# The order of two products in each group of a seven-product matmul form

## The chip, the cores and the metric

One core of a Trainium2 chip runs the whole program. Its engines work side by side, each through a list of its own: PE (TensorE, matmuls), DVE (VectorE, elementwise work), ACT (ScalarE, activations and copies), POOL (GpSimd) and SP (SyncE), of which the last two only issue transfers in the part that matters here. The metric is device microseconds of one execution, the median of several; lower is better.

## The reference

A decoder trunk of two layers over 256 tokens of width 2048, all in f32. What this case turns on are its large products with weights. Everything else (a causal convolution, eight attention heads, norms, gates) is left out here:

```python
for i in range(DEPTH):                     # DEPTH = 2
    h = rmsnorm(x, norm_mix_g[i])
    proj = h @ w_in[i]                     # 2048 columns each for the two branch gates, and more
    ...
    merged = jax.nn.sigmoid(g_conv) * y_conv + jax.nn.sigmoid(g_attn) * y_attn
    x = x + merged @ w_out[i]              # 2048 x 2048
    hf = rmsnorm(x, norm_ffn_g[i])
    gate, up = jnp.split(hf @ w_gate_up[i], 2, axis=-1)     # 2048 x 11264
    x = x + (jax.nn.silu(gate) * up) @ w_down[i]            # 5632 x 2048
    hp = rmsnorm(x, norm_ple_g[i])
    x = x + jax.nn.sigmoid(hp @ w_ple_gate[i]) * (p[i] @ w_ple_proj[i])
return rmsnorm(x, final_g)
```

## The kernel before, in words

**Tiles and splits.** Weights come from memory in raw tiles of 128 partitions by 2 x 512 f32 (512 KB, two slices of 128 inputs by 512 output columns), fetched by SP (`fetch`, L135) into eight `raw` buffers. Each f32 weight tile is split into two parts (`split`): ACT copies it in a shorter format to `wh` (L141), and DVE subtracts that from the raw tile, which leaves the rest `wl` (L142). A product of 128 inputs then takes three matmuls (`Sum.add`): inputs' high part by `wh` (L186), high part by `wl` (L187), low part by `wh` (L188). There are five `wh` and five `wl` buffers. The inputs, transposed activations, are split in the same way.

**Sums and banks.** A sum of two token blocks by 512 columns takes two banks of the accumulator, one a block. `bank_mm` gives such a pair, the name `mm` in the rows; there are two pairs, handed out in turn at the first matmul that writes them. `bank_ms` gives single banks (`ms`), of which there are four.

**Two chunks at once.** `fast_chunks` computes two neighbouring chunks of 512 columns, with weights w1 and w2. For some of the input slices (its groups, `fast`; a group is 512 inputs) it uses a form with seven products in place of eight: the two token blocks, the two chunks and the two halves of the 512 inputs form 2 x 2 matrices, the products are taken of sums of them, and the sums of weights are made by DVE on raw tiles in place (L273 adds, L274 subtracts). In the names, a11 and a12 are the first and second half of w1's group, a22 is the second half of w2's, and sm is the sum of the first halves of both, which POOL makes by an adding transfer (L277, `third`). The sums: `chain` and `q5` in single banks, c11 and c12 (token blocks 0 and 1 of the first chunk) in one pair, c21 and c22 (of the second chunk) in the other. The other input slices are multiplied plainly: each `go()` takes one raw tile, splits it and multiplies it into both blocks of the first chunk, c11 and c12, twelve matmuls; the tiles of the second chunk follow those of the first.

**The end of a call.** When all of the first chunk's `go` are done, `add(u1, u1, c1())` (L273, `pair<-pair,mm`) reads its pair and `first(u1)` uses the result. At the very end `sub(u2, c2(), u2)` (L274, `pair<-mm,pair`) reads the pair of the second chunk. The next call takes up both pairs.

**Who calls it.** The branch gates (two groups), `w_out` and `w_ple_gate` (one group for the first two chunks, two for the others), the gate and up columns of the FFN (L937, two groups, a call for each 512 columns of the hidden width but the layer's first), and `w_down` (L951; FFN in three parts per layer of 3, 4 and 4 chunks of the hidden width; one group for `n == 0`, that is columns 0 to 1023, and for `n == 2` as many as the part has `Fast` operands). 84 groups in all.

**The order of the work.** A scheduler takes the instructions as the code writes them and sets an order for each engine; a buffer's next writer waits for its last reader. On each engine the instructions then run in the order set.

Of the kernel before, what the change touches and what calls it, by code (L numbers as in the profile page):

```python
# [45 lines left out]
def trunk(ctx, tc, xT, xR, pT, wI, wF, wC, wA, wOut, wGU, wD, wPG, wPP, vec, bF, gF, out):  # L46
# [15 lines left out]
    def pair(dtype=F32):  # L62
        return pairs.tile([P, 2, 512], dtype, tag="pair", name=f"pair{next(uid)}")
# [20 lines left out]
    def run():  # L84
        for _ in range(len(turns)):
            turns.popleft()()
        if tasks:
            tasks.popleft()()

    def fill(n):  # L90
        credit[0] += n
        while background and credit[0] > 0:
            cost, op = background.popleft()
            credit[0] -= cost
            op()
        if not background:
            credit[0] = 0
# [35 lines left out]
    def fetch(src):  # L133
        raw = raws.tile([P, 2, 512], F32, tag="raw", name=f"raw{next(uid)}")
        nc.sync.dma_start(raw.rearrange("p k n -> p (k n)"), src)  # L135
        return raw

    def split(raw):
        h = whs.tile([P, 2, 512], F32R, tag="wh", name=f"wh{next(uid)}")
        l = wls.tile([P, 2, 512], F32R, tag="wl", name=f"wl{next(uid)}")  # L140
        act.activation(h, raw, AF.Copy)  # L141
        dve.tensor_tensor(l, raw, h.bitcast(F32), op=ALU.subtract)  # L142
        recent[0] = h
        return h, l
# [28 lines left out]
    class Sum:  # L173
# [8 lines left out]
        def add(self, xh, xl, wh, wl):  # L182
            start = self.left == self.n
            self.left -= 1
            kw = dict(skip_group_check=self.rest < self.n)
            pe.matmul(self.t, lhsT=xh, rhs=wh, start=start, stop=False, **kw)  # L186
            pe.matmul(self.t, lhsT=xh, rhs=wl, start=False, stop=False, **kw)  # L187
            pe.matmul(self.t, lhsT=xl, rhs=wh, start=False, stop=self.left % self.rest == 0, **kw)  # L188

    def once(make):  # L190

        made = []

        def get():
            if not made:
                made.append(make())
            return made[0]

        return get

    def sums_of_blocks(n1, n2=None):
        t = once(bank_mm)
        return t, Sum(n1, lambda: t()[:, 0, :]), Sum(n1 if n2 is None else n2, lambda: t()[:, 1, :])

    def plain(sums, xs, k0, parts, blocks=range(2)):
        h, l = parts
        for kk in range(2):
            for b in blocks:
                xh, xl = xs[k0 + kk]
                sums[b].add(xh(b), xl(b), h[:, kk, :], l[:, kk, :])  # L210

    def await_x(xs, ks):
        while not all(k in xs for k in ks):
            assert turns or tasks
            run()
# [24 lines left out]
    def fast_chunks(fast, w1, w2, xs, ks, first, by_block=None):  # L240

        nf, nk = 2 * len(fast), 4 * len(ks)
        chain, q5 = Sum(3 * nf, once(bank_ms), 3), Sum(nf, once(bank_ms))
        c1, c11, c12 = sums_of_blocks(nf + nk)
        c2, c21, c22 = sums_of_blocks(nf + nk, nk)
        if by_block is not None:
            c22 = Sum(nk, once(bank_ms))
        left = deque()  # L250
        for w, sums in ((w1, (c11, c12)), (w2, (c21, c22))):
            for g, k0 in enumerate(ks):
                for half in range(2):
                    left.append((w[len(fast) + g][:, half * 1024 : (half + 1) * 1024], sums, k0 + 2 * half))
        state = dict(quiet=True)

        def go(n=1):
            for _ in range(n):
                src, sums, k0 = left.popleft()
                parts = split(fetch(src))  # L260
                await_x(xs, (k0, k0 + 1))
                plain(sums, xs, k0, parts)
                if not state["quiet"]:
                    fill(CONV // 2 + len(left) % 2)
                    run()

        def product(to, operand, raw):
            h, l = split(raw)
            xh, xl = operand
            for kk in range(2):  # L270
                to.add(xh(kk), xl(kk), h[:, kk, :], l[:, kk, :])

        add = lambda o, a, b: dve.tensor_tensor(o, a, b, op=ALU.add)  # L273
        sub = lambda o, a, b: dve.tensor_tensor(o, a, b, op=ALU.subtract)  # L274
        def third(g):
            sm = fetch(w2[g][:, :1024])
            nc.gpsimd.dma_start(sm.rearrange("p k n -> p (k n)"), w1[g][:, :1024], accum_op=ALU.add)  # L277
            return sm

        s3 = [third(0)]  # L280
        a11s = []
        for g, f in enumerate(fast):
            a11s.append(fetch(w1[g][:, :1024]))
            product(chain, f(B11), a11s[g])
        u1 = pair()
        act.activation(u1[:, 0, :], chain.t, AF.Copy)
        for g, f in enumerate(fast):
            a11, sm = a11s[g], s3[g]
            a22, a12 = fetch(w2[g][:, 1024:]), fetch(w1[g][:, 1024:])
            product(c21, f(N4X), a22)  # L290
            go()
            product(c11, f(B21), a12)
            if len(left) > 2 * len(ks):
                go()
            if nk == 8 and len(fast) == 1:
                run()
            if g < len(fast) - 1:
                s3.append(third(g + 1))
            add(a22, sm, a22)
            product(chain, f(NT2), a22)  # L300
            if g == len(fast) - 1:
                act.activation(u1[:, 1, :], chain.t, AF.Copy)
            sub(a11, a22, a11)
            product(q5, f(M1), a11)
            add(a12, a12, a22)
            product(c12, f(B22), a12)
        for sm, f in zip(s3, fast):
            product(chain, f(T3), sm)
        add(u1[:, 1, :], u1[:, 1, :], q5.t)
        u2 = pair()  # L310
        act.activation(u2[:, 0, :], chain.t, AF.Copy)
        add(u2[:, 1, :], u2[:, 0, :], q5.t)
        state["quiet"] = False
        go(len(left) - 2 * len(ks))
        add(u1, u1, c1())
        first(u1)
        if by_block is None:
            go(len(left))
            sub(u2, c2(), u2)
            return u2  # L320
        go(len(left) - 4)
        held = [(split(fetch(src)), k0) for src, _, k0 in left]
        for b, c in enumerate((c21, c22)):
            for parts, k0 in held:
                plain([c, c], xs, k0, parts, [b])
            sub(u2[:, b, :], c.t, u2[:, b, :])
            by_block(b, u2)
# [28 lines left out]
    B11, B12, B21, B22, M1, NT2, T3, N4X = range(8)  # L356
# [203 lines left out]
    for i in range(L):  # L560
# [296 lines left out]
        def sigmoids(c, nf):  # L857

            ts = []

            def gate(t):
                for b in range(2):
                    act.activation(t[:, b, :], t[:, b, :], AF.Sigmoid, scale=norm.r(b))
                ts.append(t)

            gate(fast_chunks(norm.fast[:nf], wI[i, c], wI[i, c + 1], norm.xs, range(4 * nf, KD, 4), gate))
            return ts
# [38 lines left out]
        for n in range(0, N4, 2):  # L906
            by = (0, 1, 2, 3) if n == 0 else (0, 3, 1, 2)
            onto_x(norm, n + 1)(
                fast_chunks(
                    [fast_merged[g] for g in by[: 1 + n // 2]], *([wOut[i, m][g] for g in by] for m in (n, n + 1)),  # L910
                    merged, [4 * g for g in by[1 + n // 2 :]], onto_x(norm, n),
                )
            )
# [4 lines left out]
        for part, nch in enumerate(FFN_PARTS):  # L918
            hid = {}
            fast_hid = [Fast() for _ in range(nch - 2)]  # L920
            for c in range(c0, c0 + nch):
                w1, w2 = wGU[i, 2 * c], wGU[i, 2 * c + 1]
# [159 lines left out]
```

## Time and profile before

| | |
|---|---|
| median of three runs | 2796.34 us (2795.89 to 2798.07) |
| the profiled execution | 2801.55 us |
| its span, first to last instruction | 2799.8 us |
| granted TensorE clock | 0.997 |
| PE, DVE, ACT, POOL busy | 99%, 88%, 61%, 3% |
| weights and other transfers | 587.36 MB, mean 210 GB/s |

A row of the timeline gives the start in us, the busy time, the engine, the line of the kernel, the operation, what it writes and reads, and in brackets how long the engine was idle before and what it waited for. The names leave the buffers' numbers out. Equal instructions that follow each other stand in one row with their count, and its time runs from the first's start to the last's end. A matmul's end is modelled and overlaps the next one's start, so the pace of PE is read from starts.

### The profile page before, as it was taken

How to read it: one execution, taken by the hardware profiler on the slowest of the kernel's cores; microseconds unless marked ns; L12 is line 12 of the kernel's file. 1: busy time of each engine (PE TensorE's matmuls, PEld its weight loads, DVE VectorE, ACT ScalarE, POOL GpSimd, SP SyncE). 2: the span in 40 equal slices, each digit the busy share in tenths (PEclk: the TensorE clock that was granted, in tenths of full speed). 3: DMA queues.
4: the chain of work that ended last, by engine and by line, in shares of the span. 5: the costliest groups of instructions: out<-in, count | busy, mean ns of one | idle time of the engine just before them, and what ended most of it. 6: DMA issues, size and time to landing. Idle time of an engine off the chain costs nothing.

```text
span 2799.8 us, 35090 instructions
## 1 busy us (share of the span) xinstructions
PE 2772.3 (99%) x12544; PEld 2291.1 (82%) x12544; DVE 2475.0 (88%) x2931; ACT 1716.6 (61%) x2110; POOL 82.2 (3%) x125
## 2 busy tenths in 40 slices
PE   9999999999999999999999999999999999999998
PEld 7888888888888888888788888888887888888786
DVE  7998889878889989988869988988798898899888
ACT  7446666666556656667744466656665566566575
POOL 0000000000000000000000000000000000000000
PEclk9999999999999999999999999999999999999999
DMA  7556566666677667776655555675666777677673
GB/s 299 188 185 194 186 198 219 192 225 195 219 225 228 228 208 232 218 220 232 191 179 189 187 180 198 195 236 180 218 199 224 222 226 238 203 229 217 212 251 123
DMA packets 162176, 587.36 MB, mean 210 GB/s; under 512 B 18256, under 2 KB 18512, under 8 KB 161744
## 3 DMA queue, kind: packets, MB, share of 16 engines
q1 hardware_dynamic: 149040, 539.50, 56.0%
q0 software_dynamic: 12096, 44.05, 9.0%
q8 instruction: 98, 1.61, 0.2%
q10 hardware_dynamic: 864, 1.57, 0.2%
q14 instruction: 78, 0.64, 0.1%
HBM read 582.95 MB, written 2.10 MB: 209 GB/s over the span
## 4 chain that ended last, share of the span: by engine, by line
PE 87%; DVE 5%; DMA 4%; issue 2%; ACT 1%; SPq 0%; POOLq 0%; ACTq 0%; DVEq 0%; POOL 0%
PE mm L186 23%; PE mm L188 23%; PE mm L187 23%; PE ms L186 5%; PE ms L187 5%; PE ms L188 5%; DVE wl L142 3%; DMA raw<-in_wD_dram 2%; PE ms L349 2%; ACT wh L141 1%; DMA raw<-in_wGU_dram 1%; DVE raw L274 1%; DMA raw<-in_wI_dram 0%; PE ms L741 0%; DVE pair L274 0%
## 5 line engine op out<-in xcount | busy, mean ns | idle before, releaser
L141 ACT ACTIVATE wh<-raw 128x1024 fp32r<-128x1024 f32 x1266 | 1313.0, 1057 | 943.2 <-PE mm L188 540.5
L142 DVE TENSOR_TENSOR wl<-raw,wh 128x1024 fp32r<-128x1024 f32 x1266 | 1507.7, 1219 | 250.6 <-ACT wh L141 244.6
L186 PE MATMUL mm<-wh,pair 128*128 128x512 f32 x3184 | 1247.7, 392 | 7.9 <-DVE pair L274 7.4
L187 PE MATMUL mm<-wl,pair 128*128 128x512 f32 x3184 | 1243.0, 390 | 3.5 <-DVE wl L142 3.5
L188 PE MATMUL mm<-wh,pair 128*128 128x512 f32 x3184 | 1241.9, 390 | 0.6 <-DVE pair L340 0.5
L186 PEld LDWEIGHTS mm<-wh,pair 128*128 128x128 f32 x3184 | 598.6, 188 | 132.8 <-ACT wh L141 10.0
L188 PEld LDWEIGHTS mm<-wh,pair 128*128 128x128 f32 x3184 | 598.5, 188 | 127.4 <-DVE pair L340 1.2
L187 PEld LDWEIGHTS mm<-wl,pair 128*128 128x128 f32 x3184 | 598.6, 188 | 127.0 <-DVE wl L142 5.3
L186 PE MATMUL ms<-wh,pair 128*128 128x512 f32 x712 | 277.7, 390 | 0.0
L187 PE MATMUL ms<-wl,pair 128*128 128x512 f32 x712 | 277.1, 389 | 0.0
L188 PE MATMUL ms<-wh,pair 128*128 128x512 f32 x712 | 277.1, 389 | 0.0
L273 DVE TENSOR_TENSOR raw<-raw,raw 128x1024 f32<-128x1024 f32 x168 | 205.0, 1220 | 10.9 <-DMA raw<-in_wD_dram 8.1
L584 DVE SCALAR_TENSOR_TENSOR pair<-pair,vecs,pair 128x256 f32<-128x256 f32 x480 | 201.0, 475 | 0.0
L186 PEld LDWEIGHTS ms<-wh,pair 128*128 128x128 f32 x712 | 133.6, 188 | 28.4 <-ACT pair L1013 0.8
L187 PEld LDWEIGHTS ms<-wl,pair 128*128 128x128 f32 x712 | 133.7, 188 | 27.9 <-DVE wl L142 0.2
L188 PEld LDWEIGHTS ms<-wh,pair 128*128 128x128 f32 x712 | 133.6, 188 | 27.8
L274 DVE TENSOR_TENSOR raw<-raw,raw 128x1024 f32<-128x1024 f32 x84 | 102.5, 1220 | 1.0
L273 DVE TENSOR_TENSOR pair<-pair,ms 128x512 f32<-128x512 f32 x96 | 65.4, 681 | 10.4 <-PE ms L188 10.2
L389 DVE TENSOR_TENSOR pair<-pair,pair 128x1024 fp32r<-128x1024 f32 x52 | 63.0, 1218 | 0.0
L273 DVE TENSOR_TENSOR pair<-pair,mm 128x1024 f32<-128x1024 f32 x48 | 58.3, 1214 | 4.8 <-PE mm L188 4.8
L388 ACT ACTIVATE pair<-pair 128x1024 fp32r<-128x1024 f32 x52 | 54.6, 1059 | 8.8 <-DVE pair L379 8.1
L274 DVE TENSOR_TENSOR pair<-mm,pair 128x1024 f32<-128x1024 f32 (+1 forms) x48 | 57.9, 1206 | 1.9 <-PE mm L188 1.8
(170 smaller groups left out, 1094.7 us busy)
## 6 DMA issues: line engine op xcount, KB each, us to landing
raw<-in_wGU_dram SPq DMA_DIRECT2D x352, 512.0 KB, 5.1
raw<-in_wI_dram SPq DMA_DIRECT2D x287, 512.0 KB, 4.0
raw<-in_wD_dram SPq DMA_DIRECT2D x176, 512.0 KB, 5.7
raw<-in_wOut_dram SPq DMA_DIRECT2D x64, 512.0 KB, 5.0
raw<-in_wPG_dram SPq DMA_DIRECT2D x64, 512.0 KB, 4.9
raw<-in_wGU_dram POOLq DMA_DIRECT2D x40, 512.0 KB, 7.8
raw<-in_wA_dram SPq DMA_DIRECT2D x32, 512.0 KB, 4.8
raw<-in_wC_dram SPq DMA_DIRECT2D x32, 512.0 KB, 5.5
```

What stands on the lines that cost most here:

```text
L141: act.activation(h, raw, AF.Copy)
L142: dve.tensor_tensor(l, raw, h.bitcast(F32), op=ALU.subtract)
L186: pe.matmul(self.t, lhsT=xh, rhs=wh, start=start, stop=False, **kw)
L187: pe.matmul(self.t, lhsT=xh, rhs=wl, start=False, stop=False, **kw)
L188: pe.matmul(self.t, lhsT=xl, rhs=wh, start=False, stop=self.left % self.rest == 0, **kw)
L273: add = lambda o, a, b: dve.tensor_tensor(o, a, b, op=ALU.add)
L274: sub = lambda o, a, b: dve.tensor_tensor(o, a, b, op=ALU.subtract)
L349: pe.transpose(pt[:, kk * S + b * P : kk * S + (b + 1) * P], src(b)[:, c : c + P], ident)
L388: act.activation(h, t, AF.Copy)
L389: dve.tensor_tensor(l, t, h.bitcast(F32), op=ALU.subtract)
L584: dve.scalar_tensor_tensor(cv[c], u[c][:, j : j + S], w, cv[c], op0=ALU.mult, op1=ALU.add,)
```

## The change

Within each group, the product into c11 and one `go()` now stand ahead of the product into c21, and a second `go()`, where there is one, behind it. The two fetches change places with them. What follows (the sum a22, its product NT2, and so on) is as before.

```diff
         for g, f in enumerate(fast):
             a11, sm = a11s[g], s3[g]
-            a22, a12 = fetch(w2[g][:, 1024:]), fetch(w1[g][:, 1024:])
+            a12, a22 = fetch(w1[g][:, 1024:]), fetch(w2[g][:, 1024:])
+            product(c11, f(B21), a12)
+            go()
             product(c21, f(N4X), a22)
-            go()
-            product(c11, f(B21), a12)
             if len(left) > 2 * len(ks):
                 go()
             if nk == 8 and len(fast) == 1:
                 run()
             if g < len(fast) - 1:
                 s3.append(third(g + 1))
             add(a22, sm, a22)
             product(chain, f(NT2), a22)
             ...
             sub(a11, a22, a11)
             product(q5, f(M1), a11)
             add(a12, a12, a22)
             product(c12, f(B22), a12)
```

No instruction is added or removed on any engine; the orders of PE, ACT and DVE differ, and SP loads the two halves in the other order.

PE, at the start of the `w_down` call for columns 0 to 1023 that begins at 722 us of the profile: the end of the first product into a pair and the start of the first `go`. Before, product into c21 (`mm1191`), then the `go` into c11 and c12 (`mm1195`):

```order
L186 MATMUL mm1191_6282<-wh1189_6278,pair1100_5854 128x512
L187 MATMUL mm1191_6282<-wl1190_6279,pair1100_5854 128x512
L188 MATMUL mm1191_6282<-wh1189_6278,pair1101_5855 128x512
L186 MATMUL mm1195_6295<-wh1193_6291,pair1169_6188 128x512
L187 MATMUL mm1195_6295<-wl1194_6292,pair1169_6188 128x512
L188 MATMUL mm1195_6295<-wh1193_6291,pair1169_6188 128x512
```

Now, product into c11, then the `go`:

```order
L186 MATMUL mm1191_6282<-wh1189_6278,pair1098_5850 128x512
L187 MATMUL mm1191_6282<-wl1190_6279,pair1098_5850 128x512
L188 MATMUL mm1191_6282<-wh1189_6278,pair1099_5851 128x512
L186 MATMUL mm1191_6282<-wh1193_6291,pair1169_6188 128x512
L187 MATMUL mm1191_6282<-wl1194_6292,pair1169_6188 128x512
L188 MATMUL mm1191_6282<-wh1193_6291,pair1169_6188 128x512
```

The first product and the first `go` now write the same pair; the second pair is first written by the product into c21 after them.

DVE at the same call. `raw1187` is the tile of the first product, `raw1192` that of the `go`, `raw1188` that of the other product, `raw1181` the sum sm, `raw1182` a11; `pair1164` is the u2 of the call before. Before:

```order
L142 TENSOR_TENSOR wl1190_6279<-raw1187_6274,wh1189_6278 128x1024
L337 TENSOR_TENSOR pair1169_6188<-ms1168_6183,pair1169_6188 128x2x256
L337 TENSOR_TENSOR pair1171_6196<-ms1170_6191,pair1171_6196 128x2x256
L273 TENSOR_TENSOR raw1187_6274<-raw1181_6256,raw1187_6274 128x1024
L142 TENSOR_TENSOR wl1194_6292<-raw1192_6289,wh1193_6291 128x1024
L274 TENSOR_TENSOR raw1182_6259<-raw1187_6274,raw1182_6259 128x1024
L142 TENSOR_TENSOR wl1197_6309<-raw1188_6276,wh1196_6308 128x1024
L273 TENSOR_TENSOR raw1188_6276<-raw1188_6276,raw1187_6274 128x1024
L274 TENSOR_TENSOR pair1164_6159<-mm1124_5953,pair1164_6159 128x1024
L142 TENSOR_TENSOR wl1200_6321<-raw1198_6318,wh1199_6320 128x1024
```

Now:

```order
L142 TENSOR_TENSOR wl1190_6279<-raw1187_6274,wh1189_6278 128x1024
L142 TENSOR_TENSOR wl1194_6292<-raw1192_6289,wh1193_6291 128x1024
L142 TENSOR_TENSOR wl1196_6308<-raw1188_6276,wh1195_6307 128x1024
L273 TENSOR_TENSOR raw1188_6276<-raw1181_6256,raw1188_6276 128x1024
L274 TENSOR_TENSOR pair1164_6159<-mm1130_5982,pair1164_6159 128x1024
L142 TENSOR_TENSOR wl1200_6321<-raw1198_6318,wh1199_6320 128x1024
L939 SCALAR_TENSOR_TENSOR pair1119_5943<-pair1164_6159,rt979_5243,pair1119_5943 128x512 x2
L142 TENSOR_TENSOR wl1206_6354<-raw1188_6276,wh1205_6353 128x1024
L274 TENSOR_TENSOR raw1182_6259<-raw1188_6276,raw1182_6259 128x1024
L273 TENSOR_TENSOR raw1187_6274<-raw1187_6274,raw1188_6276 128x1024
```

Ahead of the previous call's last read of its pair (L274 into `pair1164`) there stood the sum a22, the subtraction a11 and the sum a12; now only the sum a22 does.

DVE in the second group of the gate and up call at 928 us. `raw1526` is the tile of the group's first product, `raw1527` that of the other, `raw1530` and `raw1535` those of the two `go`, `raw1518` the sum sm, `raw1500` a11. Before:

```order
L142 TENSOR_TENSOR wl1529_7915<-raw1526_7910,wh1528_7914 128x1024
L273 TENSOR_TENSOR raw1526_7910<-raw1518_7873,raw1526_7910 128x1024
L142 TENSOR_TENSOR wl1532_7927<-raw1530_7924,wh1531_7926 128x1024
L142 TENSOR_TENSOR wl1534_7943<-raw1527_7912,wh1533_7942 128x1024
L142 TENSOR_TENSOR wl1537_7955<-raw1535_7952,wh1536_7954 128x1024
L142 TENSOR_TENSOR wl1539_7972<-raw1526_7910,wh1538_7971 128x1024
L274 TENSOR_TENSOR raw1500_7797<-raw1526_7910,raw1500_7797 128x1024
L273 TENSOR_TENSOR raw1527_7912<-raw1527_7912,raw1526_7910 128x1024
L142 TENSOR_TENSOR wl1541_7984<-raw1500_7797,wh1540_7983 128x1024
```

Now:

```order
L142 TENSOR_TENSOR wl1529_7915<-raw1526_7910,wh1528_7914 128x1024
L142 TENSOR_TENSOR wl1532_7927<-raw1530_7924,wh1531_7926 128x1024
L142 TENSOR_TENSOR wl1534_7943<-raw1527_7912,wh1533_7942 128x1024
L142 TENSOR_TENSOR wl1537_7955<-raw1535_7952,wh1536_7954 128x1024
L273 TENSOR_TENSOR raw1527_7912<-raw1518_7873,raw1527_7912 128x1024
L274 TENSOR_TENSOR raw1500_7797<-raw1527_7912,raw1500_7797 128x1024
L142 TENSOR_TENSOR wl1539_7972<-raw1527_7912,wh1538_7971 128x1024
L273 TENSOR_TENSOR raw1526_7910<-raw1526_7910,raw1527_7912 128x1024
L142 TENSOR_TENSOR wl1541_7984<-raw1500_7797,wh1540_7983 128x1024
```

The sum a22 (L273 reading `raw1518`) stood second and now stands fifth, behind the splits of the other product's tile and of both `go`; the subtraction a11 has moved ahead of the split for NT2.

## The prediction, made before the changed kernel was run

> **What bounds the kernel.** I read the page's busy shares and the chain that ended last first, then what PE waited for, then the timeline around those waits, and last VectorE (DVE) at the places where the change reorders it. The span, the busy shares, the chain by engine, and three lines of PE's waits:
>
> ```profile
> span 2799.8 us, 35090 instructions
> PE 2772.3 (99%) x12544; PEld 2291.1 (82%) x12544; DVE 2475.0 (88%) x2931; ACT 1716.6 (61%) x2110; POOL 82.2 (3%) x125
> PE 87%; DVE 5%; DMA 4%; issue 2%; ACT 1%; SPq 0%; POOLq 0%; ACTq 0%; DVEq 0%; POOL 0%
> ...
> PE mm L186 <- DVE pair L274: 7.4, 4, 2.1
> PE mm L187 <- DVE wl L142: 3.5, 4, 1.6
> PE ms L349 <- DVE xt L981: 1.3, 1, 1.3
> ```
>
> PE is busy 99% of the span. The change alters no matmul count, so the most it can gain lies in PE's waits. The largest is a wait of the first matmul of a sum (L186 into `mm`) for a subtraction that reads a sum's pair of banks (L274 into `pair`): 7.4 us in four places. The first of the four, at the call of `w_down` for columns 0 to 1023 in layer 0, and then the other three and a smaller wait of the same matmul in a fifth such call:
>
> ```profile
> 726.18 0.39 PE L188 MATMUL mm<-wh,pair 128*128 128x512 f32 x1
> ...
> 727.76 0.39 PE L186 MATMUL mm<-wh,pair 128*128 128x512 f32 x1
> 728.32 1.22 DVE L273 TENSOR_TENSOR raw<-raw,raw 128x1024 f32<-128x1024 f32 x1
> 728.90 0.39 PE L188 MATMUL mm<-wh,pair 128*128 128x512 f32 x1
> 729.46 1.22 DVE L274 TENSOR_TENSOR pair<-mm,pair 128x1024 f32<-128x1024 f32 x1
> 730.82 0.47 PE L186 MATMUL mm<-wh,pair 128*128 128x512 f32 x1 [1.53 <-DVE pair L274]
> ...
> 962.21 0.47 PE L186 MATMUL mm<-wh,pair 128*128 128x512 f32 x1 [1.64 <-DVE pair L274]
> 2122.29 0.58 PE L186 MATMUL mm<-wh,pair 128*128 128x512 f32 x1 [2.14 <-DVE pair L274]
> 2353.86 0.47 PE L186 MATMUL mm<-wh,pair 128*128 128x512 f32 x1 [0.26 <-ACT wh L141]
> 2606.15 0.47 PE L186 MATMUL mm<-wh,pair 128*128 128x512 f32 x1 [2.04 <-DVE pair L274]
> ```
>
> The call before ends its last `go` at 726.18. The chain product follows, and at 727.76 the product into c21 begins: six matmuls, starts 0.228 us apart ((728.90 - 727.76) / 5). A product is thus 6 x 0.228 = 1.36 us of PE, and a `go`, with twelve, 2.72. Then PE stands: the first `go` writes c12, which lies in the pair that c11 shares, and that pair was the previous call's c2, which the subtraction u2 = c2 - u2 (L274, 729.46) has yet to read. That subtraction needs the last matmul of 726.18 only, but DVE runs the subtraction a11, a split and the sum a12 (L273, 728.32) first.
>
> **Gain A: the pair is asked for later.** The new order puts the product into c11 first, then the `go`, both in the pair that comes free early; the other pair is first touched by the product into c21. Between the previous call's last matmul and that first touch PE now has chain 1.36, product 1.36 and `go` 2.72: 5.44 us in place of 2.72. At this call the touch falls at 726.18 + 0.22 + 5.44 = 731.84. The subtraction a11 and the sum a12, 2.28 us of issue, no longer stand ahead of the reading of c2, which I put at 727.3 to 728.5; even at the old 729.46 its 1.22 us would end at 730.7. The cover exceeds the price by over 1 us, so the wait goes whole. A wait counts for the PE starts that it displaces: the last start before it is at 728.90, the next at 730.82, 1.92 instead of 0.23, so 1.69 lost where the row says 1.53; 0.16 more. Four waits: 7.4 + 4 x 0.16 = 8.0; the fifth call gives 0.26 + 0.16 = 0.4. Together 8.4 us. What is late next at these places is nothing that the trace shows: the splits for the `go` are two operations behind the first product. The bounds: no gain if the subtraction is held back beyond 731.84; 8.4 if not. I take 8.4, since less stands ahead of it than before. In `w_ple_gate`, PE waits for the last transposed input:
>
> ```profile
> 1393.57 0.66 PE L349 MATMUL ms<-ident,xt 128*128 128x128 f32 x4 [1.26 <-DVE xt L981]
> ```
>
> That operation is behind the same reading of c2 on DVE, and what moves back there is two operations of 1.14 us of issue (below), against splits that move up: at most 1.26 + 0.16 = 1.4, at least 0; I take 1.2, near the whole. All gains: 9.6 us.
>
> **Loss C: the sum a22 comes later on DVE.** In a call with two groups DVE ran, for the second group, split of a22, sum, split of the `go`'s tile, split of a12, split of the second `go`'s tile, and then the split for NT2, the subtraction, the sum a12 and the split for M1. Now the splits of a12, of the `go`'s tile, of a22 and of the second `go`'s tile come first, and the sum after them. DVE in the gate/up call at 928 us, and the matmul that needs its last split (M1):
>
> ```profile
> 925.75 3.50 DVE L142 TENSOR_TENSOR wl<-raw,wh 128x1024 fp32r<-128x1024 f32 x3
> 929.28 1.22 DVE L273 TENSOR_TENSOR raw<-raw,raw 128x1024 f32<-128x1024 f32 x1
> 930.87 2.36 DVE L142 TENSOR_TENSOR wl<-raw,wh 128x1024 fp32r<-128x1024 f32 x2 [0.36 <-ACT wh L141]
> 934.41 2.36 DVE L142 TENSOR_TENSOR wl<-raw,wh 128x1024 fp32r<-128x1024 f32 x2 [1.18 <-ACT wh L141]
> 936.69 1.22 DVE L274 TENSOR_TENSOR raw<-raw,raw 128x1024 f32<-128x1024 f32 x1
> 937.82 1.22 DVE L273 TENSOR_TENSOR raw<-raw,raw 128x1024 f32<-128x1024 f32 x1
> 939.12 2.36 DVE L142 TENSOR_TENSOR wl<-raw,wh 128x1024 fp32r<-128x1024 f32 x2
> ...
> 940.67 0.39 PE L187 MATMUL ms<-wl,pair 128*128 128x512 f32 x1
> ```
>
> Two splits in a row take 2.36, so one costs 1.14 of issue. DVE stands 1.18 us before 934.41 for ACT's copy of the second `go`'s tile, which itself arrives late: its buffer came free late. In the old order the sum (929.28) was done in front of that idle time; in the new one it is done behind it, and the idle time grows by what the sum leaves. So the splits for NT2 and M1 come 1.14 us later wherever DVE had such a wait. That DVE does not use the wait for something else is seen in the same rows: the subtraction of 936.69 has its operands since the sum of 929.28 ended at 930.50, and it still ran only after both splits. If ready work could pass work that waits, C would be nothing and the sum -9.6 alone; as these rows go, C stands. The Trainium skill, in "Perfetto Trace Analysis", section "Tensor Engine Instruction (MATMUL, LD_WEIGHTS)", says that PE can pull weight loads ahead, while ACT, DVE and GPSIMD are strictly first in, first out. The trace agrees, with the start at 936.69 against operands ready at 930.50, so the rule speaks against this change by the whole of C.
>
> In first groups the sum also moves, but DVE has no such wait there and the work up to M1 is the same: nothing lost; if the a22 sum were late there too, each would cost up to 1.14, which is rival 2. SP and POOL issue in the same places; only which half of the weights is loaded first changes, with 512 KB either way: nothing, since both halves were fetched one behind the other.
>
> How much of 1.14 reaches PE depends on the room between the split's end and the matmul. At 928 us: 939.12 + 1.22 = 940.34, due at 940.67: 0.33. The other late groups (`w_out` of both layers, two calls each of the second gate/up part of layer 0 and of both parts of layer 1):
>
> ```profile
> 470.59 2.36 DVE L142 TENSOR_TENSOR wl<-raw,wh 128x1024 fp32r<-128x1024 f32 x2
> 471.99 0.40 PE L187 MATMUL ms<-wl,pair 128*128 128x512 f32 x1
> 1185.25 0.50 PE L187 MATMUL mm<-wl,pair 128*128 128x512 f32 x1 [0.77 <-DVE wl L142]
> 1861.20 2.36 DVE L142 TENSOR_TENSOR wl<-raw,wh 128x1024 fp32r<-128x1024 f32 x2
> 1862.91 0.39 PE L187 MATMUL ms<-wl,pair 128*128 128x512 f32 x1
> 2331.06 2.36 DVE L142 TENSOR_TENSOR wl<-raw,wh 128x1024 fp32r<-128x1024 f32 x2
> 2333.70 0.39 PE L187 MATMUL ms<-wl,pair 128*128 128x512 f32 x1
> 2582.79 2.36 DVE L142 TENSOR_TENSOR wl<-raw,wh 128x1024 fp32r<-128x1024 f32 x2
> 2584.09 0.47 PE L187 MATMUL ms<-wl,pair 128*128 128x512 f32 x1
> ```
>
> Rooms, by the same subtraction: 0.18, none (PE already waits at 1185), 0.49, 1.42 and 0.08. The busy time of the engines in two of the four stretches between the late calls of a gate/up part (columns: elapsed, then PE, its loads, DVE, ACT, POOL; clock; DMA share):
>
> ```profile
> 893.20:930.60 37.40, 37.40 (x171) 31.02 (x170) 37.12 (x37) 24.93 (x28) 1.70 (x2) 1.00 0.73 220
> 2540.10:2573.90 33.80, 33.80 (x155) 28.05 (x154) 33.64 (x34) 23.58 (x28) 1.71 (x2) 1.00 0.75 227
> ```
>
> DVE has 0.28 and 0.16 us to spare there, so it cannot make up in a stretch what it lost at its start: the lateness of two calls adds up to 2.28 before the room of the second is charged. This gives 1.14 - 0.18 = 1.0 and 1.14 - 0.49 = 0.6 for `w_out`, and for the gate/up parts 2.28 - 0.33 = 1.9, 1.1 (at 1185 PE already waits for a late tile, in which I let the first call's lateness run out, and charge the second's whole), 2.28 - 1.42 = 0.9 and 2.28 - 0.08 = 2.2. Sum 7.7 us. Bounds: nothing, if the buffers that the late tiles wait for come free earlier in the new order by as much; and twice as much, 15.4, if the subtraction and the sum a12 behind the moved sum are each late by a full operation too. I take 7.7, since the rows show the wait for ACT and the order shows the sum behind it.
>
> **The sum.** -9.6 + 7.7 = -1.9 us against the profiled execution, whose own time, 2801.55, stands 5.2 above the median of the runs, 2796.34. Taken from the median: 2794.4. About 0.2% (5.6 us) is what a measurement of this kernel can tell from no change, so I forecast no change that shows.
>
> **Rivals.** First, the lateness is absorbed: the late tiles arrive earlier, because the order of last uses of the raw buffers moves too, or the gate/up parts regain it in the idle time that DVE has elsewhere. For it speaks DVE's busy share of 88%; against it the stretches above, where DVE is full. With 0 to 2 us of C left it gives 2796.34 - 9.6 + 0 to 2 = 2787 to 2789: faster. Chance 0.26.
>
> Second, slower: every second group of the gate/up calls carries the lateness to PE. The groups are counted by the summing transfers, one each, two in a call:
>
> ```profile
> raw<-in_wGU_dram POOLq DMA_DIRECT2D x40, 512.0 KB, 7.8
> ```
>
> So 20 second groups, at the split for M1, 1.14 each: 22.8, with `w_out`'s 1.6 a loss of 24.4 - 9.6 = +14.8, 2811. It shows as slower from a loss of 9.6 + 5.6 = 15.2, when 12 of the 20 pay in full. Against it stand the room of 1.42 at 2331 and that PE waits for splits in four places only (3.5 us, above). Chance 0.08.
>
> Third, the wait at the pair stays: if the subtraction u2 is now held behind more splits, the product into c21 waits as the `go` did. Then A is nothing and C remains: +7.7 - 1.2, 2803. Against it the 5.44 us of cover. Chance 0.04. That the change does nothing on the engines is out: the bank written by the first `go` differs.
>
> **How the numbers follow.** The forecast, no visible change, has 0.62; its own range is 2791 to 2798.5, from the uncertainty of the rooms and of the 1.2. Faster by over 0.2% means under 2790.7: rival one, 0.26, and a little of the forecast's edge: 0.27. Slower by over 0.2% means over 2801.9: rivals two and three, 0.11. The range of eight in ten reaches down into rival one, to 2787.5, and up to 2799.5, short of rival two.
>
> **What would show it.** In the changed kernel's waits the line of L186 for the subtraction L274 should be gone or under 1 us, and the first `go` at the `w_down` calls should follow the product without a pause. PE's waits for splits (L187 for `wl`) should have grown from 3.5 to about 10 us, mostly into `ms`, and DVE's idle time before the second `go`'s split in second groups from about 1.2 to 2.3. If the L187 waits stay near 3.5, rival one holds; if they reach 20, rival two; if L186 still waits 7 us, rival three. The forecast is wrong as a whole if PE's lost time moves by more than 5 us in total.

## The result: slower, and the profile after

The changed kernel takes 2815.07 us (median of 4 runs, 2814.84 to 2815.83), the kernel before 2796.94 in the same comparison: a ratio of 1.0065 with a 95% interval of 1.0048 to 1.0083, 18 us slower. The profiled execution of after took 2814.84 us, its median; that of before lay 5 us above its own, so the two traces differ by 13.3 us of span only. The page of after (span, busy time, the chain by engine, the splits on DVE):

```profile
span 2813.1 us, 35137 instructions
PE 2780.5 (99%) x12544; PEld 2284.9 (81%) x12544; DVE 2475.1 (88%) x2931; ACT 1711.5 (61%) x2110; POOL 82.2 (3%) x125
PE 66%; DVE 18%; DMA 6%; issue 6%; ACT 3%; ACTq 0%; DVEq 0%; SPq 0%; POOLq 0%; POOL 0%
...
L142 DVE TENSOR_TENSOR wl<-raw,wh 128x1024 fp32r<-128x1024 f32 x1266 | 1515.8, 1219 | 276.1 <-ACT wh L141 265.7
```

The row of the splits in the page of before:

```profile
L142 DVE TENSOR_TENSOR wl<-raw,wh 128x1024 fp32r<-128x1024 f32 x1266 | 1507.7, 1219 | 250.6 <-ACT wh L141 244.6
```

PE's waits in after (us in total, times, the longest):

```profile
PE mm L187 <- DVE wl L142: 7.9, 15, 1.4
PE ms L187 <- DVE wl L142: 4.9, 13, 0.6
PE ms L760 <- ACT wh L141: 1.9, 2, 1.2
PE ms L741 <- DVE pair L273: 1.3, 2, 0.9
```

The wait of L186 for L274 (7.4 us in four places) is gone. In its place PE waits for splits 28 times, 12.8 us, where it did so four times, 3.5 us. DVE was idle ahead of its splits for 276.1 us where it was 250.6. It does the same work (2475.0 and 2475.1 us), but its share of the chain has gone from 5% to 18%, DMA's from 4% to 6%, and PE's from 87% to 66%: less of the chain is now PE's own work. PE's busy time grew by 8.2 us with the same 12544 matmuls. A matmul row is 0.39 us long and the next can start 0.23 after it, so the first 0.16 us of a wait do not show as one; they lengthen the busy time, as does the longer row of the matmul behind a wait (0.50 at 938.92, below). The waits' rows add 4.6 us (14.2 before, 18.8 after, with the small lines left out here), and 8.2 + 4.6 is 12.8 of the 13.3 us.

First the gain. The `w_down` call that waited at 730.82 before, in after; the chain product, the reading of the old pair, the product into c11, and the product into c21:

```profile
730.69 0.39 PE L186 MATMUL ms<-wh,pair 128*128 128x512 f32 x1
731.66 1.22 DVE L274 TENSOR_TENSOR pair<-mm,pair 128x1024 f32<-128x1024 f32 x1
732.05 0.39 PE L186 MATMUL mm<-wh,pair 128*128 128x512 f32 x1
...
736.13 0.39 PE L186 MATMUL mm<-wh,pair 128*128 128x512 f32 x1
```

The reading ends at 732.88, and the pair is asked for at 736.13 (1.36 + 2.72 after 732.05): 3.2 us of cover. But here the reading would have been in time for the old order of products too, which asked for the pair 2.72 us after the chain product's start, at 733.41. The reading itself comes earlier: with the subtraction a11 and the sum a12 behind it, DVE starts it 0.97 us after the chain product (731.66 - 730.69), where it was 3.06 before (729.46 against 727.76 - 1.36).

Then the loss. DVE, SP and ACT in the gate/up call that starts at about 910 us. Before, the end of the first group (its second group is in the prediction):

```profile
921.05 2.35 DVE L142 TENSOR_TENSOR wl<-raw,wh 128x1024 fp32r<-128x1024 f32 x2
923.33 1.22 DVE L274 TENSOR_TENSOR raw<-raw,raw 128x1024 f32<-128x1024 f32 x1
924.46 1.21 DVE L273 TENSOR_TENSOR raw<-raw,raw 128x1024 f32<-128x1024 f32 x1
925.75 1.23 DVE L142 TENSOR_TENSOR wl<-raw,wh 128x1024 fp32r<-128x1024 f32 x1
925.75 0.33 SPq L135 DMA_DIRECT2D raw<-in_wGU_dram  x1
927.00 0.33 SPq L135 DMA_DIRECT2D raw<-in_wGU_dram  x1
929.77 2.01 ACT L141 ACTIVATE wh<-raw 128x1024 fp32r<-128x1024 f32 x2 [1.97 <-PE ms L188]
```

and after, the same and the second group:

```profile
926.63 1.21 DVE L142 TENSOR_TENSOR wl<-raw,wh 128x1024 fp32r<-128x1024 f32 x1
927.76 1.21 DVE L273 TENSOR_TENSOR raw<-raw,raw 128x1024 f32<-128x1024 f32 x1
929.01 1.23 DVE L274 TENSOR_TENSOR raw<-raw,raw 128x1024 f32<-128x1024 f32 x1
930.15 1.22 DVE L142 TENSOR_TENSOR wl<-raw,wh 128x1024 fp32r<-128x1024 f32 x1
931.29 1.22 DVE L273 TENSOR_TENSOR raw<-raw,raw 128x1024 f32<-128x1024 f32 x1
932.42 3.65 DVE L142 TENSOR_TENSOR wl<-raw,wh 128x1024 fp32r<-128x1024 f32 x3
932.58 0.33 SPq L135 DMA_DIRECT2D raw<-in_wGU_dram  x1
933.67 0.33 SPq L135 DMA_DIRECT2D raw<-in_wGU_dram  x1
936.54 2.01 ACT L141 ACTIVATE wh<-raw 128x1024 fp32r<-128x1024 f32 x2 [1.92 <-DMA raw<-in_wGU_dram]
937.64 2.36 DVE L142 TENSOR_TENSOR wl<-raw,wh 128x1024 fp32r<-128x1024 f32 x2 [1.57 <-ACT wh L141]
938.92 0.50 PE L187 MATMUL mm<-wl,pair 128*128 128x512 f32 x1 [0.45 <-DVE wl L142]
939.68 1.06 ACT L141 ACTIVATE wh<-raw 128x1024 fp32r<-128x1024 f32 x1 [1.13 <-DMA raw<-in_wGU_dram]
940.77 1.22 DVE L142 TENSOR_TENSOR wl<-raw,wh 128x1024 fp32r<-128x1024 f32 x1 [0.78 <-ACT wh L141]
941.92 1.22 DVE L273 TENSOR_TENSOR raw<-raw,raw 128x1024 f32<-128x1024 f32 x1
...
946.62 4.78 DVE L142 TENSOR_TENSOR wl<-raw,wh 128x1024 fp32r<-128x1024 f32 x4
947.89 0.50 PE L187 MATMUL ms<-wl,pair 128*128 128x512 f32 x1 [0.48 <-DVE wl L142]
```

From the split of the second `go`'s tile to the split for M1, DVE took 925.75 - 921.05 = 4.70 us before and 932.42 - 926.63 = 5.79 after: one operation more, in the first group too.

The a12 sum and the split for M1, both late by it, are the last to read the raw tiles a22 and a11, and a fetch follows the end of each. Before, SP issues one at 925.75, behind the a12 sum (924.46 + 1.21 = 925.67), and after at 932.58 (931.29 + 1.22 = 932.51); in both traces it takes 3.9 us and lands 0.10 us before ACT's copy of the second group's first `go` tile (landed at 929.67, copy at 929.77; 936.44 and 936.54). So before, too, this tile came just in time: ACT's row names a matmul that ended 0.06 us after the landing. The fetch behind the split for M1 (927.00 and 933.67) brings the second `go`'s tile: it landed 0.1 us before its copy in both traces (933.21, copy at 933.32; 939.58, copy at 939.68). The rows leave the buffers' numbers out; that these fetches take the buffers of a22 and a11 is read from the times.

From the split of the second `go`'s tile in the first group to the copy of the next `go`'s tile it was 929.77 - 921.05 = 8.72 us and is now 936.54 - 926.63 = 9.91: the one operation is passed on in full. ACT now waits for the transfer, DVE for ACT (1.57 us, and 0.78 for the second `go`) and PE for DVE (0.45 us). The second group then loses an operation again: 946.62 - 940.77 = 5.85 where the same stretch was 939.12 - 934.41 = 4.71 before, and PE waits once more, 0.48.

### The profile page after: what moved, and what is told of

Same layout as the page of the kernel before. It is cut to its first block, busy times and chain, and to the rows that moved or that the text cites. A ratio compares the mean times of both kernels' runs of the same rounds, so it can differ in the third digit from the quotient of the medians.

```text
span 2813.1 us, 35137 instructions
## 1 busy us (share of the span) xinstructions
PE 2780.5 (99%) x12544; PEld 2284.9 (81%) x12544; DVE 2475.1 (88%) x2931; ACT 1711.5 (61%) x2110; POOL 82.2 (3%) x125
## 3 DMA queue, kind: packets, MB, share of 16 engines
q10 hardware_dynamic: 864, 1.57, 0.2%
## 4 chain that ended last, share of the span: by engine, by line
PE 66%; DVE 18%; DMA 6%; issue 6%; ACT 3%; ACTq 0%; DVEq 0%; SPq 0%; POOLq 0%; POOL 0%
PE mm L187 18%; PE mm L188 18%; PE mm L186 18%; DVE wl L142 9%; DVE raw L273 4%; DMA raw<-in_wGU_dram 4%; PE ms L187 3%; PE ms L188 3%; PE ms L186 3%; ACT wh L141 3%; DMA raw<-in_wI_dram 2%; PE ms L349 1%; DVE pair L273 1%; DVE raw L274 1%; DVE pair L389 1%
## 5 line engine op out<-in xcount | busy, mean ns | idle before, releaser
L142 DVE TENSOR_TENSOR wl<-raw,wh 128x1024 fp32r<-128x1024 f32 x1266 | 1515.8, 1219 | 276.1 <-ACT wh L141 265.7
L186 PE MATMUL mm<-wh,pair 128*128 128x512 f32 x3184 | 1245.9, 391 | 0.8 <-ACT pair L339 0.7
L187 PEld LDWEIGHTS mm<-wl,pair 128*128 128x128 f32 x3184 | 598.0, 188 | 140.5 <-DVE wl L142 18.8
L186 PEld LDWEIGHTS mm<-wh,pair 128*128 128x128 f32 x3184 | 597.8, 188 | 124.4 <-ACT pair L339 1.8
L186 PE MATMUL ms<-wh,pair 128*128 128x512 f32 x712 | 278.0, 391 | 0.0
L273 DVE TENSOR_TENSOR raw<-raw,raw 128x1024 f32<-128x1024 f32 x168 | 204.6, 1218 | 0.4
L186 PEld LDWEIGHTS ms<-wh,pair 128*128 128x128 f32 x712 | 133.6, 188 | 29.3 <-ACT pair L1013 1.2
L274 DVE TENSOR_TENSOR raw<-raw,raw 128x1024 f32<-128x1024 f32 x84 | 102.7, 1223 | 2.2
L273 DVE TENSOR_TENSOR pair<-pair,ms 128x512 f32<-128x512 f32 x96 | 65.2, 679 | 1.1 <-PE ms L188 0.8
L274 DVE TENSOR_TENSOR pair<-mm,pair 128x1024 f32<-128x1024 f32 (+1 forms) x48 | 57.9, 1207 | 6.9 <-PE mm L188 6.8
L273 DVE TENSOR_TENSOR pair<-pair,mm 128x1024 f32<-128x1024 f32 x48 | 58.3, 1214 | 4.8 <-PE mm L188 4.8
```

## The experiments

Theory K, as it stood after the first four runs (theory L in the first expectations is its first half, the late sum alone): the a22 sum, which stood ahead of the waits for the `go` tiles on DVE, now stands behind the second of them; the splits after it come late, raw buffers come free late, and the next `go` tiles land late. The rivals were that the order of PE's products and banks costs (B), that the order of the fetches costs (F), and that DVE has no time to spare whatever the buffers do (S). `NEW` and `OLD` below stand for the six lines of the change after and before it.

**The new order in one-group calls only.** Twelve of the 48 calls have one group (in each layer the three of `w_down` for `n == 0`, one more of `w_down` for `n == 2`, and one each of `w_out` and `w_ple_gate`), 36 have two.

```diff
+            if len(fast) == 1:
+                NEW
+            else:
+                OLD
```

> New order only in calls with one group; calls with two groups as before. Theory L (the late sum: in two-group calls the a22 sum now stands behind a wait for the second go's tile on DVE, in both groups): the bank waits of the w_down calls go and nothing is lost, 10 us faster, about 2787. Rival B (the order of PE's products and banks itself costs, wherever it is used): the one-group calls keep their gain of 10 but pay part of the loss, 2790 to 2797. L187 waits for wl stay near 3.5 us under L.

2787.53 us, ratio 0.9962 (0.9949 to 0.9974): 9.3 us faster than before. PE's waits for splits stay at 3.3 us and the L186 wait for L274 is gone, as expected. The gain that the prediction worked out is real and can be had alone.

**The new order in two-group calls only.** The condition is `len(fast) == 2`.

> New order only in calls with two groups. Theory L: the whole loss and none of the gain: 2815 + 10 = 2825, with the bank wait L186 <- L274 of 7 us back. If gain and loss are not separable by calls: nearer to 2815.

2832.14 us, ratio 1.0115 (1.0099 to 1.0132): 35 us slower, 7 more than expected. The chain by engine:

```profile
PE 54%; DVE 23%; DMA 11%; issue 8%; ACT 4%; ACTq 0%; DVEq 0%; SPq 0%; POOLq 0%; POOL 0%
```

and PE's waits:

```profile
PE mm L187 <- DVE wl L142: 10.6, 18, 1.4
PE mm L186 <- DVE pair L274: 7.7, 4, 3.0
PE ms L187 <- DVE wl L142: 7.3, 18, 0.6
```

The bank wait is back, and PE's share of the chain is down to 54%, from 66% in the changed kernel. All of the loss comes with the 36 two-group calls: 35 / 36 = 1.0 us each on average.

**The sum ahead of the second `go`.** PE's and SP's orders as in the changed kernel; on DVE the sum is queued ahead of the second `go`'s split.

```diff
             product(c21, f(N4X), a22)
-            if len(left) > 2 * len(ks):
-                go()
+            s = add(a22, sm, a22)
+            with tc.issue_after(s.ins):
+                if len(left) > 2 * len(ks):
+                    go()
 ...
-            add(a22, sm, a22)
             product(chain, f(NT2), a22)
```

> New order everywhere, but the a22 sum is issued on DVE ahead of the second go's split, as an order on DVE alone; PE's products and SP's fetches as in the changed kernel. Theory L: the loss goes and the gain stays, 2786 to 2790, L187 waits back to 3 to 5 us. Rival B (products and banks) and rival F (the order of the two fetches): the loss stays, 2810 to 2815.

2799.60 us, ratio 1.0007 (0.9998 to 1.0015). 15 of the 18 us went, by an order on DVE alone, which speaks against B and F; but 12 us more than in one_group are left, 10 above the upper end expected.

**The old order with a late sum.** Products and fetches as before; the sum is queued on DVE behind the second `go`'s split (`last_split[0]` is the subtraction of the latest split; the lines that set it are left out).

```diff
             if len(left) > 2 * len(ks):
                 go()
+            s = last_split[0]
 ...
-            add(a22, sm, a22)
+            with tc.issue_after(s.ins):
+                add(a22, sm, a22)
```

> Old order of products and fetches, but the a22 sum is held on DVE until the second go's split (the last split of the two go) is issued. Theory L: the loss without the gain, 2815 to 2825, L187 waits of 10 us or more beside the 7 us of L186 <- L274. Rivals B and F: near 2797, as before.

2826.16 us, ratio 1.0100 (1.0086 to 1.0113). Moving the sum alone makes the kernel before 29 us slower. PE's waits in this trace (line numbers one higher):

```profile
PE mm L188 <- DVE wl L142: 13.3, 22, 0.8
PE ms L188 <- DVE wl L142: 7.2, 16, 0.6
```

The waits for splits came as expected, in 38 places, 20.5 us. The wait of 7 us at the pair, which I had expected beside them, is not there. The rows of DVE at the `w_down` call show why (L275 is the old L274, L274 the old L273):

```profile
733.68 1.22 DVE L275 TENSOR_TENSOR pair<-mm,pair 128x1024 f32<-128x1024 f32 x1 [0.40 <-PE mm L189]
...
737.29 1.22 DVE L274 TENSOR_TENSOR raw<-raw,raw 128x1024 f32<-128x1024 f32 x1
```

Holding the sum back has put the reading of the old pair ahead of all three sums, so that DVE, and not PE, waits there (0.40 us for the last matmul). So the bank wait goes without the later touch, and sum_late has that gain as well: its 29 us are the loss less the gain. With sum_forced it shows that the sum's place on DVE is what costs.

**First groups alone and second groups alone.** The conditions are `len(fast) == 2 and g == 0` and `len(fast) == 2 and g == 1`.

> New order only in the first group of calls with two groups. As the prediction had it (the late sum costs only in second groups): 2796 to 2798, as before. Theory K (carried: DVE waits for the second go's tile in first groups too, the split for M1 comes late there, and its raw buffer is what the next group's first go waits to be loaded into): 5 to 15 us slower, 2802 to 2812.

2805.56 us, ratio 1.0030 (1.0018 to 1.0041): 9 us slower (5 to 11.5 by the interval; the six runs lie between 2799.9 and 2808.7).

> New order only in the second group of calls with two groups. As the prediction had it: all of the loss that two_groups showed (35 us), 2825 to 2832. Theory K: part of it, 2812 to 2825; the two parts together about 35.

2816.84 us, ratio 1.0071 (1.0058 to 1.0085): 21 us slower. First groups do cost, which the prediction denied; second groups cost about twice as much. The two sum to 30 where both together cost 35, within the intervals (27.7 to 36.9 us for both together).

**Nine raw buffers.** The changed kernel, and the kernel before, with

```diff
-PAIRS = 28
+PAIRS = 27
-RAWS = 8
+RAWS = 9
```

> The changed kernel with nine raw buffers instead of eight (and 27 pair buffers instead of 28 to make room). Theory K: the fetch for the go no longer waits for the split for M1 of the group before, so DVE's idle time ahead of the go's splits shrinks and most of the loss goes: 2785 to 2800. Rival S (DVE has simply no time to spare, buffers do not matter): 2810 to 2816.

> The kernel before with nine raw buffers and 27 pair buffers. The bank waits stay, the rest changes little: 2790 to 2798 under both. Theory K: raws9 is no slower than this one; rival S: raws9 is about 18 us slower.

2785.27 us (ratio 0.9959, 0.9947 to 0.9972) and 2784.77 (0.9958, 0.9946 to 0.9971). With nine buffers the change costs nothing that can be measured. The timeline of DVE in the same call of raws9, the sum still behind the second `go`'s split:

```profile
923.37 7.06 DVE L142 TENSOR_TENSOR wl<-raw,wh 128x1024 fp32r<-128x1024 f32 x6
930.34 1.22 DVE L273 TENSOR_TENSOR raw<-raw,raw 128x1024 f32<-128x1024 f32 x1
931.59 1.23 DVE L274 TENSOR_TENSOR raw<-raw,raw 128x1024 f32<-128x1024 f32 x1
```

Its chain by engine:

```profile
PE 97%; issue 2%; DVE 0%; ACT 0%; POOL 0%; POOLq 0%
```

and PE's waits for splits:

```profile
PE mm L187 <- DVE wl L142: 2.8, 3, 1.4
```

Six splits follow each other without a pause, where the changed kernel had pauses of 1.57 and 0.78 us. PE is 97% of the chain, against 66% with eight buffers. The late sum is harmless when the tiles are there; so the loss needs raw buffers that come free late, and S falls. The gain has gone too: raws9_before has no wait of L186 for L274 in its trace either, though it touches the pair as early as the kernel before and has DVE's old order. The a22 sum and the reading of the old pair at the `w_down` call, first in before, then in raws9_before:

```profile
723.65 1.23 DVE L273 TENSOR_TENSOR raw<-raw,raw 128x1024 f32<-128x1024 f32 x1 [2.44 <-DMA raw<-in_wD_dram]
729.46 1.22 DVE L274 TENSOR_TENSOR pair<-mm,pair 128x1024 f32<-128x1024 f32 x1
...
720.02 1.21 DVE L273 TENSOR_TENSOR raw<-raw,raw 128x1024 f32<-128x1024 f32 x1
726.27 1.22 DVE L274 TENSOR_TENSOR pair<-mm,pair 128x1024 f32<-128x1024 f32 x1
```

Before, DVE stood 2.44 us for a transfer ahead of the sum, and some 7 us ahead of each of the other three bank waits likewise (0.96, 2.33 and 1.22 us); with nine buffers none of these waits is there. The bank wait was itself an outcome of DVE running late.

**The sum ahead of the first `go`.** On PE as in the changed kernel; a22 is split and summed ahead of the first `go`'s split on DVE.

```diff
             product(c11, f(B21), a12)
-            go()
-            product(c21, f(N4X), a22)
+            h22, l22 = split(a22)
+            s = add(a22, sm, a22)
+            with tc.issue_after(s.ins):
+                go()
+            # then the six matmuls of c21 with h22, l22
```

> PE's order of the changed kernel, but a22 is split and the a22 sum issued on DVE ahead of the first go's split, so that both waits for go tiles lie behind the sum, as in the kernel before. Theory K: what sum_forced left (12 us over one_group) goes too, 2786 to 2791. Rival (the rest is not the sum's place but the order of products or of fetches): 2798 to 2801, as sum_forced.

2792.33 us, ratio 0.9986 (0.9977 to 0.9995). 7 of the 12 us that sum_forced had left went; it is 1 us above the range expected, and 5 us over one_group stay open.

**The old order of the fetches.** The changed kernel with `a22, a12 = fetch(...), fetch(...)` as before.

> The changed kernel with the two fetches in their old order (a22, then a12); products and DVE's late sum as changed. Theory K: 2812 to 2818, as the changed kernel, since the sum still stands behind the second go's split. Rival F (the later landing of a22 is what costs): 2797 to 2805.

2821.10 us, ratio 1.0085 (1.0071 to 1.0098): 3 us above the range, as slow as the changed kernel or slower. F falls.

**27 pair buffers, eight raw ones.** The control for raws9.

> The changed kernel with 27 pair buffers and eight raw buffers: the control for raws9. Theory K: 2813 to 2817, the pair buffers do not matter. If it falls to 2800 or less, raws9 owed its gain to something other than the ninth raw buffer.

2820.52 us, ratio 1.0084 (1.0071 to 1.0096): a few us above the range, so giving up a pair buffer costs if anything, and the gain of raws9 is the ninth raw buffer's.

**Nine raw buffers and the new order in one-group calls.**

> Nine raw buffers and 27 pair buffers with the new order in one-group calls only. Theory K: nothing is left for the change to gain or lose with nine buffers, 2784 to 2786, as raws9 and raws9_before. If the two gains add (12 from the buffer, 9 from the one-group calls): 2775 to 2778.

2785.49 us, ratio 0.9959 (0.9947 to 0.9972): the two gains do not add. The three versions with nine raw buffers lie within 0.7 us of each other, 11 to 12 us below the kernel before: the order makes no difference that can be measured there.

## Why the prediction was wrong

**Gain A (9.6 us): the size right, the reason in part.** The waits are gone, and one_group measured 9.3. That the sizes meet is in part luck: 9.6 was read from a trace that lay 5 us above its median, and from that trace to one_group's it is 14.0 us of span (2799.8 to 2785.8). Nor was the later touch of the pair needed everywhere: at the `w_down` call shown the earlier reading is enough, and sum_late lost the bank waits with the old touch. The prediction had the earlier reading as a help only. What it did not see is that a late DVE, and with it the raw buffers, stood behind those waits. The 1.2 for `w_ple_gate` came in part: of the wait of 1.3 us, 0.9 is left in one_group's trace.

**Loss C (7.7 us): the right start, mis-sized by a factor of more than four.** two_groups measured 35. The late sum is what costs, but the way from it to PE was another. Two steps failed.

The first is "nothing lost" for first groups. That DVE has no pause there is so in the rows of before; but it means that one operation moved behind the second `go`'s split comes straight off the lead of the a12 sum and the split for M1, and these free the buffers of the second group's `go` tiles. Measured: 9 us in first_only.

The second is the charge per place against the room at the matmul. I took each of six places, subtracted its room, and let lateness run out between them. The room at the matmul was not what counted: the a12 sum and the split for M1 also free raw buffers, and the `go` tiles that are loaded into them landed, even before, only 0.1 us ahead of ACT's copy. From there lateness goes round: sum and split, buffer, transfer, copy, split. So the idle time before the second `go`'s split did not grow from 1.2 to 2.3 us, as foretold: in the call shown it is 0.78, and 1.57 us stand before the first `go`'s, where it was 0.36. And PE pays not in six places: if each matmul's start in after is held against the one of the same number in before, PE falls back by 0.3 to 1.9 us in 24 of the 36 two-group calls, and by less or nothing in the rest. Measured: 21 us in second_only, and nothing left with a ninth buffer. (The two places called `w_out`, at 470 and 1861 us, lie in branch gate calls: POOL issues the first `w_out` transfers of the two layers at 489.9 and 1880.5 us, and in after the `w_out` calls lose nothing.) The listed waits for splits came out at 12.8 us, near the 10 foretold; they understate what PE lost.

**Rival two** had the mechanism's reach and nearly the time (2811), with a chance of 0.08. Its count was the second groups of the gate/up calls; in truth first groups took part too, and other two-group calls than those of the FFN. That its time came so near is in part luck: its loss was 24.4 us, where two_groups measured 35. I spoke against it with four places in which PE waited for splits before, but a trace without late sums cannot show how many places lie just short of waiting. Rival one (lateness absorbed) needed what the ninth buffer gave. Rival three fell with the L186 line.

**That DVE runs its list in order, whatever is ready,** held: in the second group of after the sum had its operands when the split of a22 ended (937.64 + 2.36 = 940.00), and still DVE stood 0.78 us and ran the second `go`'s split first. The size of the loss did not follow from it.

**What stays open.** one_group's gain and two_groups' loss add to +26 us, where the change itself cost 18; intervals of some 4 us on each cover part of it. Waits for splits are 17.9 us in the trace of two_groups and 12.8 in that of after, so the new order of the one-group calls seems to spare the two-group calls some of theirs; no run shows how. Nor is it settled what the last 5 us of sum_first are.

## What to carry to other kernels

When an operation moves on an in-order engine from in front of a wait to behind it, charge its whole time to everything that follows, and ask which buffer each of the late operations frees: if the tile that the engine waits for next is loaded into that buffer, the lateness goes round and can be paid again in each iteration, whatever the room at the next matmul. Before moving the order of a loop that is this tight, try one more buffer: here it was worth at least as much as the best order (2785 against 2788 us), and made the order irrelevant. And a rival that differs from the forecast only in how often a price is paid deserves a chance as large as the count is uncertain.

## What the runs showed that I had not expected

The first 0.16 us of a wait between two matmuls do not appear as a wait, and the matmul behind it has a longer row: the changed kernel's PE busy time is 8.2 us longer for the same 12544 matmuls, more than what its listed waits grew by (4.6 us). A sum of listed waits was thus a lower bound for what PE lost here.
